# Left sums of a Strassen-type down-projection: on VectorE instead of accumulating transfers

## The chip, the cores and the metric

The kernel runs on one core of one Trainium2 chip. The metric is device microseconds of one execution, the median of three runs. One more execution was taken with the hardware profiler; its trace gives every row shown here.

## The reference, cut to what matters

One decoder block over 1024 tokens of width 1024 (`D_FF` is 2816), all in float32. The change lies in its last step, the down-projection of the gated MLP:

```python
h = rmsnorm(x, norm_ffn_g[l])
u = causal_dwconv(jnp.einsum("bsd,df->bsf", h, w_up[l]), conv_ffn_w[l])
gate_f, up_f = u[..., :D_FF], u[..., D_FF:]
x = x + jnp.einsum("bsf,fd->bsd", jax.nn.silu(gate_f) * up_f, w_down[l])
...
return rmsnorm(x, norm_final_g)
```

## The kernel before, in words

The kernel builds its instruction streams with a small list scheduler of its own: `Flow.run` holds threads, each of which yields the next instruction for one engine with a guessed duration and a rank; of the instructions that are ready when an engine comes free, the one of the lowest rank is emitted. What is emitted is then the fixed order of each engine's queue. Semaphores are set by the framework from that order, so an engine waits at an instruction until its inputs are there, and everything behind it in the same queue waits too.

`ffn_up` (up to line 1883) makes the 22 blocks of silu(gate) * up, each 128 features by 1024 tokens. ScalarE does the Silu (L1843), GpSimd multiplies by up (L1844), and SyncE stores the block in `act_dram` (L1846).

`ffn_down` multiplies those activations by `w_down`. It takes the 22 blocks in three groups of 6, 8 and 8. In a group the two operands are cut into 2 by 2 quarters, and the 8 quarter products are replaced by 7 products of sums of quarters (Strassen's method in Winograd's form). A quarter is 128 partitions by m feature blocks by 512, m being 3, 4 and 4 in the three groups, so it has 1536 or 2048 elements per partition.

- The left quarters come from the activations: A and B for the first 512 tokens, C and D for the last 512. The right quarters E, F, G, H come from `w_down`.
- The left sums are s1 (of C and D), s3 (of C and A), s2 (of A and s1) and s4 (of B and s2). The right sums are t1 to t4.
- The products are p1 = (A, E), p2 = (B, G), p6 = (s2, t2), p7 = (s3, t3), p5 = (s1, t1), p4 = (D, t4), p3 = (s4, H). TensorE does them in this order in every group (`order`, L1901). Before a product both factors are cut in two float32r parts (high and low): ScalarE copies the high part (L2031), VectorE subtracts it from the source for the low one (L2032), for two feature blocks at a time (1024 elements; 512 for the odd third block of the first group). The cut operands lie in `ht`, four places per side, that is two products' worth.
- A product is three matmuls (L374 to L376: low x high, high x high, high x low) per feature block and per 128 tokens: 36 matmuls in the first group and 48 in the others, 924 in all. The third of the three is the only one that reads the right factor's low part.
- The result of p1 is copied to the other four banks of PSUM before p2 adds to it (`seed`, L2080). Finished quarters are copied to the residual tiles x2 by ScalarE in the first group (L2091) or added to them by VectorE (L2096).

Right sums are made by VectorE (`rights`, L2004 and L2005). Left sums are made by transfers that add into their target, all from GpSimd's queue: `loaded` adds the second quarter to the one just loaded from DRAM (s1 and s3, L1979), and `lefts` adds s1 into the tile of A for s2, and s2 into the tile of B for s4 (L1988). Such a target can only be overwritten after its own cut. Loads of quarters go through SyncE's queue (L1971).

The block's own residual input is also added by accumulating transfers from GpSimd's queue: `residual` (L1945) has 16, of 256 KB each, one for each quarter of 128 tokens, and issues them while the first group runs. `finish` and `part` at the end of the kernel take the sum of squares, the final gain and the store.

Of the kernel before, what the change touches and what calls it, by code (L numbers as in the profile page):

```python
# [12 lines left out]
ALU = mybir.AluOpType  # L13
# [4 lines left out]
P = 128  # L18
# [4 lines left out]
H = 8  # L23
# [238 lines left out]
class Block:  # L262
# [1621 lines left out]
    def ffn_down(self, flow):  # L1884
# [13 lines left out]
        last = len(groups) - 1  # L1898
        x2, blocks, ops = [], {}, {}
        halves = [slice(0, 512), slice(512, 1024)]  # L1900
        order = ("p1", "p2", "p6", "p7", "p5", "p4", "p3")  # L1901
        base = dict(p1=0, p2=0, p6=4, p7=0, p5=4, p4=0, p3=4)
        target = dict(p2=(0, 0), p6=(4, 0), p7=(4, 1), p5=(4, 1), p4=(4, 0), p3=(0, 1))
        factors = dict(p1=("A", "E"), p2=("B", "G"), p6=("s2", "t2"), p7=("s3", "t3"), p5=("s1", "t1"), p4=("D", "t4"), p3=("s4", "H"))
# [32 lines left out]

        def residual():

            for p in ("p2", "p5", "p4", "p3"):  # L1940
                s0, half = target[p]
                for j in range(4):
                    yield On(("used", p, 0, j))
                    c = halves[half]
                    yield pool(1.0, lambda: gpsimd.dma_start(out=x2[s0 + j][:, c], in_=self.x2_dram[s0 + j][:, c], accum_op=ALU.add))  # L1945
                    flow.post(("x2", s0 + j, half), 4.0)
# [14 lines left out]

        def loads():
            for n, (_, _, m) in enumerate(groups):
                for name, (ready, src), more in (("A", left(n, 0, 0), None), ("E", right(n, 0, 0), None), ("B", left(n, 0, 1), None),
                                                 ("G", right(n, 1, 0), None), ("F", right(n, 0, 1), None), ("H", right(n, 1, 1), None),
                                                 ("s1", left(n, 1, 0), left(n, 1, 1)), ("s3", left(n, 1, 0), left(n, 0, 0)),
                                                 ("D", left(n, 1, 1), None)):
                    x = yield Get("blk")
                    t = self.m(f"blk{x}", P, m, 512)
                    yield On(*ready, *(more[0] if more else []))  # L1970
                    yield sp(0.75 * m, lambda: nc.sync.dma_start(out=t, in_=src))  # L1971
                    blocks[n, name] = x, t
                    flow.post(("load", n, name))
                    flow.fork(loaded(n, name, t, more), 0)

        def loaded(n, name, t, more):
# [3 lines left out]
                yield 4.0  # L1980
            flow.post(("block", n, name))

        def lefts(n):

            for to, x, y in (("s2", "A", "s1"), ("s4", "B", "s2")):
                yield On(("cut", n, x), ("block", n, y))
                o, src = blocks[n, x], blocks[n, y][1]
                yield pool(1.0, lambda: gpsimd.dma_start(out=o[1], in_=src, accum_op=ALU.add))  # L1988
                blocks[n, to] = o
                flow.post(("added", n, to))  # L1990
                yield 4.0
                flow.post(("block", n, to))

        def rights(n):
            m = groups[n][2]

            def op(to, o, x, y, fn):
                a, b = blocks[n, x][1], blocks[n, y][1]
                yield dve(512 * m, lambda: fn(o[1], a, b))
                blocks[n, to] = o  # L2000
                flow.post(("added", n, to))
                flow.post(("block", n, to))

            minus = lambda o, a, b: vector.tensor_tensor(out=o, in0=a, in1=b, op=ALU.subtract)  # L2004
            both = lambda o, a, b: vector.scalar_tensor_tensor(out=o, in0=a, scalar=-1.0, in1=b, op0=ALU.mult, op1=ALU.subtract)  # L2005
            yield On(("block", n, "F"), ("block", n, "H"))
            x = yield Get("blk")
            yield from op("t3", (x, self.m(f"blk{x}", P, m, 512)), "H", "F", minus)
            yield On(("block", n, "E"))
            yield from op("t1", blocks[n, "F"], "E", "F", minus)  # L2010
            yield On(("cut", n, "E"))
            yield from op("t2", blocks[n, "E"], "t1", "H", both)
            yield On(("cut", n, "G"), ("block", n, "G"))
            yield from op("t4", blocks[n, "G"], "t2", "G", both)


        later = dict(A="s2", B="s4", E="t2", G="t4")
# [1 line left out]

        def cuts(side):  # L2020
            for n, (_, _, m) in enumerate(groups):
                for p in order:
                    name = factors[p][side]
                    for k0 in range(0, m, 2):
                        x = yield Get(f"op{side}")
                        k = slice(k0, min(k0 + 2, m))
                        w = k.stop - k0
                        both = self.m(f"op{side}{x}", P, 2, 2, 512, dt=F32R)
                        yield On(("block", n, name))
                        src = blocks[n, name][1][:, k]  # L2030
                        yield act(w * 512, lambda: scalar.copy(out=both[:, 0, :w], in_=src))  # L2031
                        yield dve(w * 512, lambda: vector.tensor_tensor(out=both[:, 1, :w], in0=src, in1=f(both[:, 0, :w]), op=ALU.subtract))  # L2032
                        ops[n, p, k0, side] = x, both
                        flow.post(("op", n, p, k0, side))
# [15 lines left out]

        def products():
            for n, (_, _, m) in enumerate(groups):
                for p in order:
                    units = range(0, m, 2)
                    finest = n == last and p == "p3"
                    steps = [(k0, j) for j in range(4) for k0 in units] if finest else [(k0, j) for k0 in units for j in range(4)]
                    for k0, j in steps:
                        yield On(("op", n, p, k0, 0), ("op", n, p, k0, 1))
                        if k0 == 0:
                            yield On(bank_free(n, p, j))  # L2060
                        l, r = (ops[n, p, k0, side][1] for side in range(2))
                        ps = self.psum[:, base[p] + j, :]
                        w = min(2, m - k0)

                        def emit():
# [17 lines left out]
        def add(n, p, j):  # L2083

            s, half = target[p]
            s += j
            ps = self.psum[:, base[p] + j, :]
            if n == 0 and p in ("p2", "p6", "p7", "p3"):
                yield On("x2 places")
                o = x2[s][:, halves[half]]  # L2090
                yield act(540, lambda: scalar.activation(out=o, in_=ps, func=AF.Copy, scale=1.0 if s < 4 else -1.0))  # L2091
            else:
                if n:
                    yield On(("x2", s, half))
# [20 lines left out]

        def part(s, half, p, o, ss):
            ns = halves[half]
            yield On(("used", p, last, s % 4), "gain", *([("used", "p7", last, s % 4)] if s > 3 else []))
            flow.fork(squares(s, half, ss), 1)
            yield dve(560, lambda: vector.tensor_tensor(out=o[:, ns], in0=x2[s][:, ns], in1=self.gf[:, ns], op=ALU.mult))  # L2120
            yield On(("squares", s, half))
            flow.post(("part", s, half))
# [14 lines left out]

        def sides():
            for n in range(len(groups)):
                flow.fork(lefts(n), 1)  # L2140
                flow.fork(rights(n), 4 + n)
            yield 0.0

        def finishes():
            yield On(("used", "p7", last, 3))
            for s in (4, 5, 6, 7, 0, 1, 2, 3):
                flow.fork(finish(s), 2.5)

# [54 lines left out]
```

## Time and profile before

| what | value |
|---|---|
| median of three runs (2035.25 to 2039.29) | 2036.22 us |
| the profiled execution, as timed | 2038.57 us |
| its span from first to last instruction | 2036.8 us |
| TensorE busy, share of the span | 1982.9 us, 97% |
| VectorE busy | 1350.5 us, 66% |
| ScalarE busy | 906.2 us, 44% |
| GpSimd busy | 415.2 us, 20% |
| mean granted clock of TensorE | 0.988 of full speed |
| down-projection, first matmul to last | 1787.57 to 2029.35 us |
| software DMA queue (GpSimd's) | 22.81 MB, 5.1% of 16 engines |

Times in the trace are microseconds from the span's start. PE is TensorE, DVE VectorE, ACT ScalarE, POOL GpSimd, SP SyncE; a "q" behind an engine's name means its instruction queue. A tile is shown by the memory region that it lies in, not by its name in the program: of the left quarters of the first group A lies in `s5`, B in `s4`, C in `s3`, D in `w`; of the right ones E lies in `raw`, G in `s5`, F in `sb`, H in `s0`. A matmul's recorded duration includes its way through the array, so the next one starts before it ends; the step from start to start is what counts.

### The profile page before, as it was taken

Reading aid. Unit: us, or ns where it says so; the run is one execution under the profiler, and the core shown is the slowest. Engines: PE = TensorE matmul, PEld = TensorE weight load, DVE = VectorE, ACT = ScalarE, POOL = GpSimd, SP = SyncE. Lnnn points to the kernel's source line nnn. Section 1 sums busy time; section 2 is a strip of 40 time slices with the busy share of each in tenths; the row PEclk is TensorE's granted clock in tenths of the full one; section 3 lists DMA queues with packets and bytes.
Section 4 is the critical chain, followed back from the end, with each engine's and each line's share of the span. In section 5 each row is a group of like instructions: output and inputs, shape, how many; then the busy total and the mean of one; then the engine's idle time right before and its main releaser. Section 6 shows DMA issues by size and latency. Waiting matters only on the chain.

```text
span 2036.8 us, 27849 instructions
## 1 busy us (share of the span) xinstructions
PE 1982.9 (97%) x10645; PEld 1659.6 (81%) x10645; DVE 1350.5 (66%) x2488; ACT 906.2 (44%) x1936; POOL 415.2 (20%) x347
## 2 busy tenths in 40 slices
PE   9999999999999999999999999989999999968998
PEld 8987888888888888888888888867888888856787
DVE  7378678779778744666666332567777776756767
ACT  5265364464464334555454111344443443433435
POOL 3132021121120001010000022014445435322001
PEclk9999999999999999999999999999999999989999
DMA  6022311312312332101115543222322222299722
GB/s 213 33 75 50 90 43 47 86 40 49 85 40 50 104 116 72 36 26 37 56 47 180 163 135 106 91 73 73 109 72 88 89 73 91 76 278 247 212 58 83
DMA packets 204233, 187.99 MB, mean 92 GB/s; under 512 B 43418, under 2 KB 166020, under 8 KB 203588
## 3 DMA queue, kind: packets, MB, share of 16 engines
q1 hardware_dynamic: 189012, 150.75, 24.0%
q0 software_dynamic: 8032, 22.81, 5.1%
q10 hardware_dynamic: 7056, 12.65, 1.7%
q8 instruction: 84, 1.38, 0.3%
q14 instruction: 49, 0.40, 0.1%
HBM read 138.74 MB, written 41.68 MB: 89 GB/s over the span
## 4 chain that ended last, share of the span: by engine, by line
PE 90%; DMA 4%; DVE 3%; ACT 1%; issue 1%; POOL 0%; SPq 0%; POOLq 0%; ACTq 0%
PE psum L391 32%; PE psum L374 12%; PE psum L376 12%; PE psum L375 12%; PE psum L1394 5%; PE psum L489 3%; PE psum L1403 3%; DMA s<-s 2%; PE psum L1348 2%; PE psum L1568 1%; PE psum L1571 1%; PE psum L1570 1%; PE psum L679 1%; DMA s<-act_dram 1%; PE psum L871 1%; PE psum L905 1%
## 5 line engine op out<-in xcount | busy, mean ns | idle before, releaser
L391 PE MATMUL psum<-ht,w 128*128 128x512 f32 x2688 | 688.1, 400 | 0.1
L391 PEld LDWEIGHTS psum<-ht,w 128*128 128x128 f32 x2688 | 486.1, 189 | 89.8 <-DVE ht L1418 0.5
L374 PE MATMUL psum<-ht 128*128 128x512 f32 x308 | 122.2, 397 | 26.7 <-DVE ht L2032 15.0
L1860 DVE SCALAR_TENSOR_TENSOR s<-psum,cols,s 128x1023 f32<-128x1023 f32 (+1 forms) x88 | 106.8, 1275 | 54.7 <-ACT s L1857 54.7
L376 PE MATMUL psum<-ht 128*128 128x512 f32 x308 | 121.6, 395 | 0.3 <-DVE ht L2032 0.3
L375 PE MATMUL psum<-ht 128*128 128x512 f32 x308 | 121.6, 395 | 0.0
L636 DVE SCALAR_TENSOR_TENSOR s<-psum,cols,s 128x511 f32<-128x511 f32 (+1 forms) x144 | 105.3, 740 | 5.0 <-ACT s L631 4.8
L2032 DVE TENSOR_TENSOR ht<-s,ht 128x1024 fp32r<-128x1024 f32 (+1 forms) x60 | 66.7, 1139 | 51.0 <-ACT ht L2031 51.0
L2031 ACT CAST ht<-s 128x1024 fp32r<-128x1024 f32 (+1 forms) x60 | 57.0, 988 | 88.1 <-PE psum L376 53.6
L1844 POOL TENSOR_TENSOR s<-s 128x1024 f32<-128x1024 f32 x22 | 53.3, 2425 | 209.4 <-ACT s L1843 209.4
L374 PEld LDWEIGHTS psum<-ht 128*128 128x128 f32 x308 | 59.0, 192 | 39.8 <-DVE ht L2032 15.4
L766 DVE TENSOR_TENSOR s<-sc,s 64x240 f32<-64x240 f32 (+27 forms) x248 | 85.7, 346 | 5.6 <-DMA sc<-md_dram 1.1
L768 DVE TENSOR_TENSOR s<-s 64x240 f32<-64x240 f32 (+27 forms) x248 | 80.0, 323 | 5.9
L1857 ACT ACTIVATE s<-psum,cols 128x1024 f32<-128x1024 f32 x44 | 46.7, 1113 | 70.0 <-PE psum L376 70.0
L1328 DVE TENSOR_REDUCE nm<-psum 128x1 f32<-128x256 f32 (+5 forms) x64 | 48.3, 756 | 41.6 <-PE psum L1395 41.6
L374 PE MATMUL psum<-ht,w 128*128 128x512 f32 x168 | 66.4, 395 | 7.1 <-DVE w L1768 3.8
L623 DVE TENSOR_TENSOR w<-raw,w 128x512 fp32r<-128x512 f32 x96 | 65.4, 685 | 10.5 <-ACT w L621 10.4
L374 PE MATMUL psum<-ht,s 128*128 128x512 f32 x184 | 71.7, 390 | 0.4 <-DVE s L1768 0.4
L376 PE MATMUL psum<-ht,s 128*128 128x512 f32 x184 | 71.6, 389 | 0.0
L375 PE MATMUL psum<-ht,s 128*128 128x512 f32 x184 | 71.6, 389 | 0.0
L1483 POOL TENSOR_TENSOR s<-s 128x1024 f32<-128x1024 f32 x4 | 13.2, 3288 | 286.0 <-DMA rx<-in_w_o_mla_dram 260.6
L391 PE MATMUL psum<-s,w 128*128 128x512 f32 x288 | 69.9, 391 | 0.0
(456 smaller groups left out, 4742.4 us busy)
## 6 DMA issues: line engine op xcount, KB each, us to landing
raw<-in_w_in_dram SPq DMA_DIRECT2D x48, 512.0 KB, 4.2
raw<-in_w_up_dram SPq DMA_DIRECT2D x22, 512.0 KB, 3.7
act_dram<-s SPq DMA_DIRECT2D x22, 512.0 KB, 2.7
s<-in_x_dram SPq DMA_DIRECT2D x16, 512.0 KB, 3.6
sg_dram<-s ACTq DMA_DIRECT2D x16, 512.0 KB, 2.7
s<-sg_dram SPq DMA_DIRECT2D x16, 512.0 KB, 3.7
s<-act_dram SPq DMA_DIRECT2D x8, 1024.0 KB, 6.1
rx<-in_w_up_dram SPq DMA_DIRECT2D x11, 512.0 KB, 4.9
```

The source lines that it names most:

```text
L374: self.nc.tensor.matmul(ps, lhsT=ll, rhs=rh, start=first, stop=False, **kw)
L375: self.nc.tensor.matmul(ps, lhsT=lh, rhs=rh, start=False, stop=False, **kw)
L376: self.nc.tensor.matmul(ps, lhsT=lh, rhs=rl, start=False, stop=last, **kw)
L391: product = lambda o, l, r, **kw: pe(0.2155, lambda: self.nc.tensor.matmul(o, lhsT=l[:, k, :], rhs=r, **kw))
L489: yield pe(0.000417 * (b - a), lambda: tensor.matmul(ps[:, u, :b - a], lhsT=l[:, k, cs], rhs=w[:, k, a:b], start=n == 0, stop=n == 3 * KD ...
L623: yield dve(512, lambda: nc.vector.tensor_tensor(out=lo[:, c], in0=raw[:, c], in1=f(hi[:, c]), op=ALU.subtract))
L636: yield dve(570, lambda: nc.vector.scalar_tensor_tensor(out=o, in0=src[:, max(a - d, 0):b - d], scalar=self.cw[:, n, j:j + 1], in1=o, op0= ...
L766: yield dve(n * w, lambda: nc.vector.tensor_tensor(out=t, in0=mb[:, j, j + 1:].unsqueeze(2).to_broadcast(sh), in1=xb[:, j, :w].unsqueeze(1 ...
L768: yield dve(n * w, lambda: nc.vector.tensor_tensor(out=xb[:, j + 1:, :w], in0=xb[:, j + 1:, :w], in1=t, op=ALU.subtract))
L1394: nc.tensor.matmul(ps[:, n, :w], lhsT=l, rhs=r[:, n * w:(n + 1) * w], start=t == 0, stop=t == len(terms) - 1 and n != parts - 1)
L1860: yield dve(1160, lambda: vector.scalar_tensor_tensor(out=acc[:, d:], in0=src[:, :S - d], scalar=self.cf[:, n, j:j + 1], in1=acc[:, d:], o ...
L2032: yield dve(w * 512, lambda: vector.tensor_tensor(out=both[:, 1, :w], in0=src, in1=f(both[:, 0, :w]), op=ALU.subtract))
```

## The change

In the first group, C is loaded as it is, and VectorE makes all four left sums: s3 into a place of its own, s1 in place of C, s2 in place of A, s4 in place of B. In the other two groups s1 and s3 are still made by the accumulating transfers of `loaded`, and VectorE makes s2 and s4. The first group's product order becomes p1, p2, p7, p6, p5, p4, p3. The residual transfers start one group later: those of three quarters after the second group's last addition to that quarter, those of the fourth after p6 of the last group. Additions to x2 wait for them only in the last group, and `part` waits for them by name.

```diff
-        order = ("p1", "p2", "p6", "p7", "p5", "p4", "p3")
+        order = lambda n: ("p1", "p2", "p6", "p7", "p5", "p4", "p3") if n else ("p1", "p2", "p7", "p6", "p5", "p4", "p3")
...
-            for p in ("p2", "p5", "p4", "p3"):
-                s0, half = target[p]
+            for p, n, quarter in (("p2", last - 1, "p2"), ("p5", last - 1, "p5"), ("p3", last - 1, "p3"), ("p6", last, "p4")):
+                s0, half = target[quarter]
                 for j in range(4):
-                    yield On(("used", p, 0, j))
+                    yield On(("used", p, n, j))
...
+                sums = (("C", left(n, 1, 0), None),) if n == 0 else (("s1", left(n, 1, 0), left(n, 1, 1)), ("s3", left(n, 1, 0), left(n, 0, 0)))
...
+        def sum_steps(n, to, o, x, y, fn):
+            a, b = blocks[n, x][1], blocks[n, y][1]
+            yield dve(512 * groups[n][2], lambda: fn(o[1], a, b))
+            blocks[n, to] = o
+            flow.post(("added", n, to))
+            flow.post(("block", n, to))
...
         def lefts(n):
 
-            for to, x, y in (("s2", "A", "s1"), ("s4", "B", "s2")):
-                yield On(("cut", n, x), ("block", n, y))
-                o, src = blocks[n, x], blocks[n, y][1]
-                yield pool(1.0, lambda: gpsimd.dma_start(out=o[1], in_=src, accum_op=ALU.add))
...
+            if n == 0:
+                yield On(("block", n, "C"), ("block", n, "D"))
+                x = yield Get("blk")
+                yield from sum_steps(n, "s3", (x, self.m(f"blk{x}", P, groups[n][2], 512)), "C", "A", plus)
+                yield from sum_steps(n, "s1", blocks[n, "C"], "C", "D", plus)
+            yield On(("cut", n, "A"), ("block", n, "s1"), ("block", n, "s3"))
+            yield from sum_steps(n, "s2", blocks[n, "A"], "A", "s1", plus)
+            flow.fork(sum_after(n, "s4", "B", "s2", "B", plus), 7 + n)
...
-                if n:
+                if n == last and p != "p2" and not (p == "p6"):
                     yield On(("x2", s, half))
...
-            yield On(("used", p, last, s % 4), "gain", *([("used", "p7", last, s % 4)] if s > 3 else []))
+            yield On(("used", p, last, s % 4), ("x2", s, half), "gain", *([("used", "p7", last, s % 4)] if s > 3 else []))
...
-                flow.fork(lefts(n), 1)
+                flow.fork(lefts(n), 4 + n)
...
-            yield On(("used", "p7", last, 3))
+            yield On(("used", "p7", last, 3), ("used", "p6", last, 3))
```

VectorE's queue at the start of the first group, before. In the order of the rows: t3; the low part of G's first piece (`ht` from `s5`, 1024); t1; the low part of G's second piece (512); t2; t4; and the cuts of p6's factors, s2 (`s5`) and t2 (`raw`), which were reached by way of two transfers.

```order
L2004 TENSOR_TENSOR s2_13927<-s0_13911,sb_13896 128x1536
L2032 TENSOR_TENSOR ht_78<-s5_9852,ht_78 128x1024
L2004 TENSOR_TENSOR sb_13896<-raw_66,sb_13896 128x1536
L2032 TENSOR_TENSOR ht_78<-s5_9852,ht_78 128x512
L2005 SCALAR_TENSOR_TENSOR raw_66<-sb_13896,s0_13911 128x1536
L2005 SCALAR_TENSOR_TENSOR s5_9852<-raw_66,s5_9852 128x1536
L2032 TENSOR_TENSOR ht_78<-raw_66,ht_78 128x1024
L2032 TENSOR_TENSOR ht_78<-raw_66,ht_78 128x512
L2032 TENSOR_TENSOR ht_78<-s5_9852,ht_78 128x1024
```

The same place in the changed kernel, where sums are lines 1990 to 1992 and cuts line 2035:

```order
L1991 TENSOR_TENSOR s2_13927<-s0_13911,sb_13896 128x1536
L2035 TENSOR_TENSOR ht_78<-s5_9852,ht_78 128x1024
L1991 TENSOR_TENSOR sb_13896<-raw_66,sb_13896 128x1536
L1990 TENSOR_TENSOR w_13929<-s3_13928,s5_9852 128x1536
L1992 SCALAR_TENSOR_TENSOR raw_66<-sb_13896,s0_13911 128x1536
L1990 TENSOR_TENSOR s3_13928<-s3_13928,w_13929 128x1536
L2035 TENSOR_TENSOR ht_78<-s5_9852,ht_78 128x512
L1990 TENSOR_TENSOR s5_9852<-s5_9852,s3_13928 128x1536
L2035 TENSOR_TENSOR ht_78<-w_13929,ht_78 128x1024
L2035 TENSOR_TENSOR ht_78<-s2_13927,ht_78 128x1024
L1992 SCALAR_TENSOR_TENSOR s5_9852<-raw_66,s5_9852 128x1536
L2035 TENSOR_TENSOR ht_78<-w_13929,ht_78 128x512
```

Three sums (s3, t2, s1) now stand between t1 and the low part of G's second piece, which p2 needs, and a fourth (s2) stands between that and the first cuts of p7 (s3 in `w`, t3 in `s2`).

GpSimd's queue over the same time, before; L1979 and L1988 are the accumulating transfers of the left sums, L1945 those of the residual:

```order
L1979 DMA s3_13928<-act_dram_10711 128x3x512
L1844 TENSOR_TENSOR s4_9851<-s4_9851 128x1024
L1979 DMA w_13929<-act_dram_10711 128x3x512
L1988 DMA s5_9852<-s3_13928 128x1536
L1945 DMA s1_13930<-x2_dram_10710 128x512 x2
L1988 DMA s4_9851<-s5_9852 128x1536
L1945 DMA s1_13930<-x2_dram_10710 128x512 x2
L1979 DMA s3_13928<-act_dram_10711 128x4x512
L1945 DMA s1_13930<-x2_dram_10710 128x512 x2
L1945 DMA sc_13897<-x2_dram_10710 128x512
```

And in the changed kernel, from the last two products of `ffn_up` on:

```order
L1844 TENSOR_TENSOR s4_9851<-s4_9851 128x1024 x2
L1979 DMA sb_13896<-act_dram_10711 128x4x512
L1979 DMA w_13929<-act_dram_10711 128x4x512
L1945 DMA s1_13930<-x2_dram_10710 128x512 x4
L1979 DMA s5_9852<-act_dram_10711 128x4x512
L1945 DMA s1_13930<-x2_dram_10710 128x512
L1979 DMA s5_9852<-act_dram_10711 128x4x512
```

The two transfers of the second group's s1 and s3 stand directly behind the last product, with no residual transfer ahead of them.

## Rows read from the trace of the kernel before

**Rows 1.** Groups by line, 1786 to 2037 us: busy, mean ns, idle before, releasers

```profile
L374 PE MATMUL psum<-ht 128*128 128x512 f32 x308 | 122.2, 397 | 26.7 <-DVE ht L2032 15.0 <-ACT psum L2080 11.7
```

**Rows 2.** Timeline of TensorE: start, us, line, shape, [idle before <-releaser]

```profile
1787.57 0.39 PE L374 MATMUL psum<-ht 128*128 128x512 f32 x1
...
1796.63 0.50 PE L376 MATMUL psum<-ht 128*128 128x512 f32 x1 [0.28 <-DVE ht L2032]
...
1802.20 0.39 PE L376 MATMUL psum<-ht 128*128 128x512 f32 x1
...
1804.24 0.39 PE L376 MATMUL psum<-ht 128*128 128x512 f32 x1
...
2029.35 0.39 PE L376 MATMUL psum<-ht 128*128 128x512 f32 x1
```

**Rows 3.** Chain of work that ended last: start, us, what

```profile
1795.77 7.55 DMA s<-act_dram
...
1803.89 13.39 DMA s<-s
...
1859.97 23.39 DMA s<-s
```

**Rows 4.** Timeline of VectorE, first group, and one row of the second

```profile
1793.69 1.75 DVE L2004 TENSOR_TENSOR s<-s,sb 128x1536 f32<-128x1536 f32 x1
1795.36 1.22 DVE L2032 TENSOR_TENSOR ht<-s,ht 128x1024 fp32r<-128x1024 f32 x1
1796.49 4.67 DVE L2004 TENSOR_TENSOR sb<-raw,sb 128x1536 f32<-128x1536 f32 x1
1801.08 0.68 DVE L2032 TENSOR_TENSOR ht<-s,ht 128x512 fp32r<-128x512 f32 x1
1801.68 1.75 DVE L2005 SCALAR_TENSOR_TENSOR raw<-sb,s 128x1536 f32<-128x1536 f32 x1
1803.46 1.76 DVE L2005 SCALAR_TENSOR_TENSOR s<-raw,s 128x1536 f32<-128x1536 f32 x1
...
1855.94 4.62 DVE L2032 TENSOR_TENSOR ht<-s,ht 128x1024 fp32r<-128x1024 f32 x4
```

**Rows 5.** Timeline of GpSimd, two of the products of `ffn_up`

```profile
1775.80 2.41 POOL L1844 TENSOR_TENSOR s<-s 128x1024 f32<-128x1024 f32 x1 [10.18 <-ACT s L1843]
...
1796.65 2.89 POOL L1844 TENSOR_TENSOR s<-s 128x1024 f32<-128x1024 f32 x1
```

**Rows 6.** Timeline of ScalarE: the last Silu, and the cut behind the second wait

```profile
1794.42 1.06 ACT L1843 ACTIVATE s<-s 128x1024 f32<-128x1024 f32 x1
...
1883.46 1.99 ACT L2031 CAST ht<-s 128x1024 fp32r<-128x1024 f32 x2 [16.84 <-DMA s<-s]
```

**Rows 7.** Timeline of TensorE, two waits long before, at the start of `ffn_up`

```profile
1359.12 0.50 PE L374 MATMUL psum<-ht,w 128*128 128x512 f32 x1 [2.63 <-ACT psum L1796]
...
1367.04 0.47 PE L374 MATMUL psum<-ht,w 128*128 128x512 f32 x1 [3.77 <-DVE w L1768]
```

**Rows 8.** Busy by stretch: PE, PEld, DVE, ACT, POOL (x), granted clock, DMA share, GB/s

```profile
1364.00:1368.00 4.00, 0.96 (x4) 0.86 (x5) 3.96 (x4) 0.00 (x0) 2.27 (x2) 1.00 0.29 87
1368.10:1371.40 3.30, 3.30 (x9) 2.24 (x7) 2.58 (x6) 0.62 (x1) 0.00 (x0) 0.50 0.42 125
```

**Rows 9.** Line 2004 by shape: duration ns min/median/max, first and last start

```profile
L2004 DVE TENSOR_TENSOR sb<-w,s x1: 2292/2292/2292, 1838.6 to 1838.6; 128x2048 f32<-128x2048 f32 x1
```

**Rows 10.** Timeline of SyncE's queue: the load of the second group's C

```profile
1833.87 0.37 SPq L1971 DMA_DIRECT2D s<-act_dram  x1
```

**Rows 11.** Timeline of GpSimd: the transfer that adds D to it

```profile
1841.65 1.30 POOL L1979 DMA_DIRECT2D s<-act_dram  x1 [21.20 <-DMA s<-act_dram]
```

**Rows 12.** DMA issues, 1787 to 1900 us: KB each, median us from issue to landing

```profile
s<-x_dram POOLq DMA_DIRECT2D x12, 256.0 KB, 15.6
...
s<-act_dram POOLq DMA_DIRECT2D x1, 1024.0 KB, 9.1
```

**Rows 13.** VectorE busy in 20 us of the last group

```profile
1937.00:1957.00 20.00, 16.62 (x17) 1.00 0.37 73
```

More of the change, by code (lines that the diff above doesn't have):

```diff
@@ L1963, in loads @@
             for n, (_, _, m) in enumerate(groups):
+                sums = (("C", left(n, 1, 0), None),) if n == 0 else (("s1", left(n, 1, 0), left(n, 1, 1)), ("s3", left(n, 1, 0), left(n, 0, 0)))
                 for name, (ready, src), more in (("A", left(n, 0, 0), None), ("E", right(n, 0, 0), None), ("B", left(n, 0, 1), None),
-                                                 ("G", right(n, 1, 0), None), ("F", right(n, 0, 1), None), ("H", right(n, 1, 1), None),
-                                                 ("s1", left(n, 1, 0), left(n, 1, 1)), ("s3", left(n, 1, 0), left(n, 0, 0)),
+                                                 ("G", right(n, 1, 0), None), ("F", right(n, 0, 1), None), ("H", right(n, 1, 1), None), *sums,
                                                  ("D", left(n, 1, 1), None)):
@@ L1981, in loaded @@
             flow.post(("block", n, name))
-        def lefts(n):
-            for to, x, y in (("s2", "A", "s1"), ("s4", "B", "s2")):
-                yield On(("cut", n, x), ("block", n, y))
-                o, src = blocks[n, x], blocks[n, y][1]
-                yield pool(1.0, lambda: gpsimd.dma_start(out=o[1], in_=src, accum_op=ALU.add))
[L1989 to L1992, printed above, removed]
-        def rights(n):
[L1995 to L2005, printed above, removed]
+        def sum_steps(n, to, o, x, y, fn):
[4 more added lines that the diff above has]
+            flow.post(("block", n, to))
@@ new lines, in ffn_down @@
+        plus = lambda o, a, b: vector.tensor_tensor(out=o, in0=a, in1=b, op=ALU.add)
+        minus = lambda o, a, b: vector.tensor_tensor(out=o, in0=a, in1=b, op=ALU.subtract)
+        both = lambda o, a, b: vector.scalar_tensor_tensor(out=o, in0=a, scalar=-1.0, in1=b, op0=ALU.mult, op1=ALU.subtract)
+        def lefts(n):
+            if n == 0:
[6 more added lines that the diff above has]
+            flow.fork(sum_after(n, "s4", "B", "s2", "B", plus), 7 + n)
@@ L2006, in rights, with sum_after @@
+        def sum_after(n, to, x, y, waits, fn):
+            yield On(("cut", n, waits), ("block", n, x), ("block", n, y))
+            yield from sum_steps(n, to, blocks[n, waits], x, y, fn)
+        def rights(n):
             yield On(("block", n, "F"), ("block", n, "H"))
             x = yield Get("blk")
-            yield from op("t3", (x, self.m(f"blk{x}", P, m, 512)), "H", "F", minus)
+            yield from sum_steps(n, "t3", (x, self.m(f"blk{x}", P, groups[n][2], 512)), "H", "F", minus)
@@ L2009, in rights @@
             yield On(("block", n, "E"))
-            yield from op("t1", blocks[n, "F"], "E", "F", minus)
+            yield from sum_steps(n, "t1", blocks[n, "F"], "E", "F", minus)
             yield On(("cut", n, "E"))
-            yield from op("t2", blocks[n, "E"], "t1", "H", both)
-            yield On(("cut", n, "G"), ("block", n, "G"))
-            yield from op("t4", blocks[n, "G"], "t2", "G", both)
+            yield from sum_steps(n, "t2", blocks[n, "E"], "t1", "H", both)
+            flow.fork(sum_after(n, "t4", "t2", "G", "G", both), 7 + n)
@@ L2021, in cuts @@
             for n, (_, _, m) in enumerate(groups):
-                for p in order:
+                for p in order(n):
                     name = factors[p][side]
@@ L2052, in products @@
             for n, (_, _, m) in enumerate(groups):
-                for p in order:
+                for p in order(n):
                     units = range(0, m, 2)
```

## The prediction

> **What bounds the kernel now.** I read the groups by line first: the 308 matmuls of L374 that read `ht` from both sides, with as many of L375 and L376, are the 924 of the down-projection, and all that TensorE waited before them is 26.7 us, 15.0 for one cut of VectorE and 11.7 for one copy of ScalarE [rows 1]. Then the timeline of TensorE: between 1802.20 and 1804.24 lie 9 matmuls, so a step is 0.2267 us. The first down-projection matmul starts at 1787.57, the last at 2029.35 [rows 2], 241.8 us apart, while 923 steps take 209.2. So 32.5 us are lost in this stage: the 26.7, 0.3 at 1796.63, and about 5.5 of matmuls at the lower clock level after the two waits. What follows the last matmul is one tail of 7 us, which the change leaves alone.
>
> The chain of waits says where the two waits come from. For p6 of the first group, s1 is made by a transfer of 7.55 us and s2 by one of 13.39, one after the other [rows 3]; TensorE stands from 1804.47 to 1819.66. In the second group the transfer that makes s2 takes 23.39 us [rows 3], and ScalarE's cut of it [rows 6] stands in ScalarE's queue ahead of the four copies of p1 without which p2 can't start. TensorE bounds all the rest.
>
> **The change part by part.** Removed: all six transfers that make s2 and s4, the two that made s1 and s3 of the first group, and one load there (C, which was loaded twice). Both links of the first chain and the one of the second are among them. Added: eight sums on VectorE, four of 1536 and four of 2048 elements. A 1536 sum steps 1.67 us (1793.69 to 1795.36), its form with a scalar 1.78 and 1.68, a cut of 1024 elements 1.13, one of 512 0.60 [rows 4]; a 2048 sum takes 2.29 [rows 9]. I follow VectorE's new queue from 1793.69, before which nothing differs.
>
> t3 steps to 1795.36 and the low part of G's first piece to 1796.49, as now. t1 comes next. It now takes 4.67 us where its like takes 1.75, and it is the one sum that runs beside a GpSimd product [rows 4, 5]; it lost 2.9 us. That product still comes at this place, right behind the Silu that ends at 1795.48 [rows 6], and without the transfer that stands ahead of it now. Its 2.4 us [rows 5] are all that t1 can lose. From 1796.49 that gives 1796.49 + 2.4 + 1.7 = 1800.6 for t1's end. Then s3, t2 and s1 take 1.67 + 1.78 + 1.67 = 5.1, to 1805.7; C has landed by 1795.77 now, where the transfer that adds to it starts [rows 3], and D is loaded right behind it, so neither is late. Only then comes the low part of G's second piece, done at 1806.4. Now it starts at 1801.08 and is done at 1801.76 [rows 4], just ahead of the matmul at 1802.20 that reads it [rows 2], the third of p2's second piece. **So the change puts a new wait of 4.2 us into p2.** The ten matmuls left of p2 end at 1808.7. VectorE goes on with s2 (1.67, from 1806.3), the cut of s3 (done at 1809.2) and that of t3, done at 1810.3. p7's first matmul needs the one, its third the other, so the third starts at 1810.3.
>
> From there I find no further wait. p7 runs to 1818.0. Until then VectorE makes t4 (1.7), two cuts of 512 (1.2), s4 (1.7) and the cuts of s2 and t2 (2.3), to 1817.2; the second of these is needed 0.45 us after p6's start. This is the thinnest place. ScalarE empties p2's banks one by one as they end, before p7 comes to them, and p6's likewise before p5; I cost that at nothing, its queue being short here.
>
> In the second group s1 is still a transfer. C's load needs the place of t1, which is cut by 1823.4; load to issue of the transfer takes 7.8 us now [rows 10, 11] and the transfer 9.1 [rows 12], so s1 is there at 1840.3. VectorE comes to s2 at 1848 (p4's additions and the cuts of A and E stand ahead). s2 is ready at 1850.3, p6 starts at 1872.4; the wait for 23.39 is gone with its transfer. The third group has more time still. The residual moves behind p2, p5 and p3 of the second group and p6 of the last; its transfers took 15.6 us [rows 12], and p4's additions to the last quarter come 29 us after p6's. I cost it at nothing; that cover gone, each microsecond later delays the tail by one.
>
> **The sum.** p7's third matmul is number 75; 849 steps of 0.2267 follow it, 192.5 us. The last matmul starts at 1810.3 + 192.5 = 2002.8 against 2029.35: 26.6 us less. From it goes the lower clock. A wait of 3.77 us at 1367.04 [rows 7] was followed by 3.3 us at a granted 0.50, which began 1 us after TensorE had resumed [rows 8]; one of 2.63 [rows 7] had no such stretch behind it. Nine matmuls at half speed cost 1.8 us at most, and nothing while they wait for VectorE anyway, as p2's end does. I take 0.5, with bounds 0 and 1.8. That leaves 26.1 us. The profiled execution's 2038.57 becomes 2012.5; the median is 2.35 below it, so **2010 us**.
>
> Which of the two engines has the way to SBUF first is open. In the row, t1 started at 1796.49, 0.16 us before the product, and still lost 2.9 us [rows 4, 5]. By that, the product that starts at 1795.6 may also stop the cut that began at 1795.36; p2's third matmul would then wait 2.3 us longer, and the later wait shrinks to 1.9, because VectorE's total is the same. Two short waits, no lower clock: 2009.5. The Trainium skill ("SBUF — State Buffer", "SBUF: two separate sides") says that VectorE and GpSimd share a port pair as an exclusive lock, kept for the whole instruction by whichever starts first. By that rule the cut would end undisturbed, and there is one wait of 4.2 us: 2010. The row of t1 speaks against the second half of the rule.
>
> **The rivals.**
> First, VectorE's sums are all as slow as t1 was: s3, t2 and s1 each lose 2.9 us before G's second piece, 8.7 in all, and the clock costs its 1.8 in full: 2010 + 8.7 + 1.3 = 2020. It would take GpSimd work on SBUF between 1800 and 1806. For it: t1's row. Against it: GpSimd's new queue has nothing between the last product and the second group's transfers.
>
> Second, the wait moves into the second group: the transfer of s1 comes late, and VectorE stands at s2 with p2's cuts behind it. s2, t2 and two cuts take 2.3 + 2.3 + 2.3 us and p2 starts at 1861.5, so it decides from a landing at 1854.6, 23 us after its issue at 1831.2. For it: one transfer has taken 23.39 [rows 3]. Against it: that one stood behind residual transfers, this one behind none. Each microsecond beyond costs one; 5 would give 2015.
>
> Third, the other side: VectorE becomes the bound of the last two groups and the kernel is slower than before. In its densest stretch there VectorE is busy 16.62 of 20 us [rows 13]. A group is 7 products of 48 steps, 76.2 us, so 63.3 of work; with two more sums 67.9. Both groups together have 16.6 us to spare. To be slower than before it must grow by 16.6 + 26 = 43 us. That takes a loss like t1's 2.9 us at 15 of its instructions; the candidates are GpSimd's 20 transfers there, each if it blocked VectorE for 2.1 us while it is issued. Against it: four cuts took 4.62 us, 1.15 each and so undisturbed, while GpSimd issued a whole row of transfers at 1855.94 [rows 4]. Time if it all came: 2040.
>
> **How the numbers follow.** Forecast 0.85; first rival 0.06; second 0.04; third 0.03. The remaining 0.02 is for no difference: the gain found again as some wait that I don't see. About 0.2%, 4 us, is what a measurement of this kernel can tell from no change; the three runs lie 4 us apart. Faster by more than that: forecast and the first two rivals, 0.95; same 0.02; slower 0.03. The lower end: had t1 lost nothing, 2.4 us less, 2007.6; with the lowest run 1 us below the median, and 0.5 of clock given back, 2006. The upper end: full clock cost (1.3), p6's thin place missed by 2, highest run 3 above the median, 2016; and to take in most of the first rival, 2019.
>
> **What would show it.** Right: TensorE's two long waits gone, one of about 4 us for VectorE at 1802 to 1806 in p2, one of half a microsecond at p7; the last matmul about 26 us earlier; no L1988 transfers, s2 of the second group on VectorE before 1855. Wrong: a wait above 1 us for `ht` after p7 of the first group, a TensorE wait for ScalarE's copies (L2083), a sum other than t1 above 2.5 us, or a tail over 8 us.

## The result and the profile after

The changed kernel took 2013.18 us (median of four runs, 2011.96 to 2014.35), the kernel before 2037.76 beside it (2035.25 to 2040.40): a ratio of 0.9879, 95% interval 0.9862 to 0.9896. The profiled execution took 2012.15 us, its span is 2010.4.

The groups by line, the answer to [rows 1]: the 26.7 us of waiting before L374 are gone, and 4.0 stand before L376, all of it for cuts by VectorE (0.28 of it stood there before too [rows 2]).

```profile
L376 PE MATMUL psum<-ht 128*128 128x512 f32 x308 | 121.3, 394 | 4.0 <-DVE ht L2035 4.0
```

TensorE's timeline, the answer to [rows 2]:

```profile
1786.33 0.39 PE L374 MATMUL psum<-ht 128*128 128x512 f32 x1
...
1800.78 0.39 PE L375 MATMUL psum<-ht 128*128 128x512 f32 x1
1804.87 0.80 PE L376 MATMUL psum<-ht 128*128 128x512 f32 x1 [3.70 <-DVE ht L2035]
1805.46 0.63 PE L374 MATMUL psum<-ht 128*128 128x512 f32 x1
1805.89 0.63 PE L375 MATMUL psum<-ht 128*128 128x512 f32 x1
...
1810.15 0.62 PE L376 MATMUL psum<-ht 128*128 128x512 f32 x1
1810.58 0.43 PE L374 MATMUL psum<-ht 128*128 128x512 f32 x1
...
2002.87 0.39 PE L376 MATMUL psum<-ht 128*128 128x512 f32 x1
```

From the first down-projection matmul to the last are 216.54 us, 25.2 less than before. The stage also began 1.24 us earlier, which the change cannot touch (in e5, the same kernel again, it began at 1788.89). There is one new wait, in p2 (a step of 4.09 us), and twelve matmuls behind it step 0.43 us instead of 0.2267: the lower clock. The busy time by stretch (TensorE, its weight loads, VectorE, ScalarE, GpSimd, then the granted clock) shows it from 1803.8 on:

```profile
1786.30:1803.80 17.50, 14.58 (x63) 11.37 (x61) 16.12 (x10) 8.60 (x11) 3.27 (x1) 1.00 0.76 274
1803.80:1810.60 6.80, 5.73 (x14) 4.48 (x15) 6.62 (x6) 2.85 (x6) 0.00 (x0) 0.50 0.30 114
```

VectorE's timeline, the answer to [rows 4], holds the row of sums that makes TensorE wait, and s2 of the second group:

```profile
1794.12 1.22 DVE L2035 TENSOR_TENSOR ht<-s,ht 128x1024 fp32r<-128x1024 f32 x1
1795.26 3.95 DVE L1991 TENSOR_TENSOR sb<-raw,sb 128x1536 f32<-128x1536 f32 x1
1799.13 1.74 DVE L1990 TENSOR_TENSOR w<-s,s 128x1536 f32<-128x1536 f32 x1
1800.80 1.75 DVE L1992 SCALAR_TENSOR_TENSOR raw<-sb,s 128x1536 f32<-128x1536 f32 x1
1802.46 1.74 DVE L1990 TENSOR_TENSOR s<-s,w 128x1536 f32<-128x1536 f32 x1
1804.13 0.68 DVE L2035 TENSOR_TENSOR ht<-s,ht 128x512 fp32r<-128x512 f32 x1
...
1807.54 1.21 DVE L2035 TENSOR_TENSOR ht<-s,ht 128x1024 fp32r<-128x1024 f32 x1
1808.68 1.75 DVE L1992 SCALAR_TENSOR_TENSOR s<-raw,s 128x1536 f32<-128x1536 f32 x1
...
1847.97 2.28 DVE L1990 TENSOR_TENSOR s<-s,sb 128x2048 f32<-128x2048 f32 x1
```

Only t1 is long, and GpSimd's last product of `ffn_up` stands beside it (timeline of GpSimd, the answer to [rows 5]):

```profile
1794.32 3.27 POOL L1844 TENSOR_TENSOR s<-s 128x1024 f32<-128x1024 f32 x1 [17.35 <-ACT s L1843]
```

### The profile page after: what moved, and what is told of

Its sections match the earlier page's. It is cut to its first block, busy times and chain, and to the rows that moved or that the text cites. A ratio compares the mean times of both kernels' runs of the same rounds, so it can differ in the third digit from the quotient of the medians.

```text
span 2010.4 us, 27839 instructions
## 1 busy us (share of the span) xinstructions
PE 1978.5 (98%) x10645; PEld 1655.8 (82%) x10645; DVE 1363.8 (68%) x2496; ACT 907.3 (45%) x1936; POOL 409.1 (20%) x339
## 4 chain that ended last, share of the span: by engine, by line
PE 92%; DVE 4%; DMA 1%; ACT 1%; issue 1%; POOL 0%; SPq 0%; POOLq 0%; ACTq 0%; DVEq 0%
PE psum L391 32%; PE psum L374 12%; PE psum L376 12%; PE psum L375 12%; PE psum L1394 5%; PE psum L489 3%; PE psum L1403 3%; PE psum L1348 2%; PE psum L1568 1%; PE psum L1571 1%; PE psum L1570 1%; PE psum L679 1%; PE psum L871 1%; PE psum L905 1%; PE psum L915 1%; PE psum L873 1%
## 5 line engine op out<-in xcount | busy, mean ns | idle before, releaser
L376 PE MATMUL psum<-ht 128*128 128x512 f32 x308 | 121.3, 394 | 4.0 <-DVE ht L2035 4.0
L374 PE MATMUL psum<-ht 128*128 128x512 f32 x308 | 120.8, 392 | 0.0
L374 PE MATMUL psum<-ht,w 128*128 128x512 f32 x168 | 66.3, 395 | 7.1 <-DVE w L1768 3.8
L376 PEld LDWEIGHTS psum<-ht 128*128 128x128 f32 x308 | 58.5, 190 | 17.1 <-DVE ht L2035 4.8
L374 PE MATMUL psum<-ht,s 128*128 128x512 f32 x184 | 71.7, 390 | 0.4 <-DVE s L1768 0.4
L376 PE MATMUL psum<-ht,s 128*128 128x512 f32 x184 | 71.6, 389 | 0.0
```

What stands on the lines that cost most here:

```text
L374: self.nc.tensor.matmul(ps, lhsT=ll, rhs=rh, start=first, stop=False, **kw)
L376: self.nc.tensor.matmul(ps, lhsT=lh, rhs=rl, start=False, stop=last, **kw)
```

## The experiments

They ran on several chips, each beside the kernel before. "Stage" is the time from the first to the last matmul of the down-projection in the profiled execution: 241.78 us before, 216.54 after, so it leaves out what varies ahead of it. The kernel before has one profile, from one chip; so a stage's gain and the gain in time beside that run differ by up to 3.3 us (e2).

| run | us | ratio to before, 95% | stage, us |
|---|---|---|---|
| e1: only s2, s4 of groups 2 and 3 on VectorE | 2027.59 | 0.9931 (0.9917 to 0.9946) | 230.13 |
| e2: only the first group's part | 2043.81 | 1.0010 (1.0001 to 1.0020) | 247.11 |
| e3: only the residual later | 2027.06 | 0.9925 (0.9911 to 0.9940) | 229.07 |
| e4: the change, residual early | 2026.42 | 0.9925 (0.9910 to 0.9940) | 228.89 |
| e5: the change, again | 2014.23 | 0.9882 (0.9864 to 0.9901) | 216.43 |
| e6: the change, VectorE waits for the product | 2012.40 | 0.9868 (0.9854 to 0.9883) | 215.68 |
| e7: e4 with that wait | 2014.45 | 0.9876 (0.9862 to 0.9891) | 216.84 |
| e8: cuts first on VectorE | 2015.56 | 0.9882 (0.9868 to 0.9897) | 218.24 |
| e9: cuts first on VectorE and ScalarE | 2007.87 | 0.9846 (0.9833 to 0.9860) | 210.67 |
| e10: e2 with the wait of e6 | 2027.06 | 0.9941 (0.9928 to 0.9955) | 230.71 |
| e11: e4 again | 2013.13 | 0.9888 (0.9864 to 0.9912) | 216.39 |
| e12: e6 with p6 ahead of p7 | 2013.43 | 0.9868 (0.9852 to 0.9885) | 217.40 |

### Parts of the change alone: e1 to e4

e1, on the kernel before:

```diff
...
-                yield pool(1.0, lambda: gpsimd.dma_start(out=o[1], in_=src, accum_op=ALU.add))
+                if n == 0:
+                    yield pool(1.0, lambda: gpsimd.dma_start(out=o[1], in_=src, accum_op=ALU.add))
+                else:
+                    yield dve(512 * groups[n][2], lambda: plus(o[1], o[1], src))
...
-                flow.fork(lefts(n), 1)
+                flow.fork(lefts(n), 4 + n if n else 1)
```

> The kernel before, with only s2 and s4 of the second and third group made on VectorE; the first group keeps its two transfers, its order of products and its four sums by transfer, and the residual transfers stay where they were. Theory (the two gains are separate, each is its chain's): the second wait of 11.7 us, behind the transfer of 23.39, goes, and with it about 2 us of lower clock behind it; the wait of 15.0 us in the first group stays. So 13 to 14 us under the kernel before, about 2023, and the first group's waits unchanged within 0.5 us. Rival (the residual transfers are what is late): s1 of the second group, still a transfer behind residual transfers, now holds VectorE at s2, and a wait of more than 2 us stands at the second group's start: gain under 10 us.

e2 has all lines of the change's diff that concern `n == 0`, `loads`, `lefts` and the order, and none of those in `residual` and `add`; `lefts` of the later groups is as before.

> The kernel before, with only the first group's part of the change (C loaded as it is, four sums on VectorE, p7 ahead of p6); groups 2 and 3 make s2 and s4 by transfers, the residual transfers stay early. Theory: the first wait of 15.0 us and its lower clock of about 3 us go, and the changed kernel's own wait of 4.0 us in p2 and its lower clock of about 3 us come: 11 us under the kernel before, and the second wait stays at 8 to 14 us, because s2's transfer still stands behind twelve residual transfers. Rival: without the first wait everything ahead of the second group's s2 is earlier too, and the second wait shrinks below 5 us: 18 us or more under the kernel before.

e3 has only the lines of the diff in `residual`, `add`, `part` and `finishes`.

> The kernel before, with only the residual transfers moved one group later; all left sums are still transfers. Theory A (the 23.39 us of s2's transfer are mostly waiting behind residual transfers in the same queue): it takes about 9 us here, like the one of 1024 KB in the rows of before, and the second wait of 11.7 us goes: 11 to 14 us under the kernel before, as much as the VectorE sums of these two groups give. Theory B (the transfer from SBUF to SBUF is slow in itself): it takes over 18 us again and the wait stays above 6 us: under 6 us gained.

e4, on the changed kernel, takes those same lines of `residual` and `add` back.

> The changed kernel, with the residual transfers back where they were, one group earlier. Theory (the prediction's: VectorE's sums take the transfers out of the chain, the residual's place costs nothing either way): within 1.5 us of the changed kernel, 2013; s1 of the second group lands up to 1854, just in time. Rival: s1's transfer now stands behind the residual transfers and lands after 1855; VectorE waits at s2 with p2's cuts behind it, and TensorE waits 3 to 12 us at the second group: 2016 to 2025.

In e1 the second wait is gone and the time 14.2 us less, as expected; the first wait, which was to stay within 0.5 us, grew by 2.4. e3 did nearly as much, 14.7 us: the second group's s2 is still a transfer there, but with no residual transfer ahead of it in the queue it takes 10.6 us instead of 23.4 [rows 3], and the wait for it is gone (DMA issues of e3):

```profile
s<-s POOLq DMA_DIRECT2D x1, 1024.0 KB, 10.6
```

So the two parts are two cures for the same wait, and they do not add up. e2 and e4 went wrong: e2 gained nothing, e4 lost 12 us of stage against the change. Both show one thing that no theory of mine had, a GpSimd product of 21.91 us. In e4, GpSimd's timeline:

```profile
1796.90 21.91 POOL L1844 TENSOR_TENSOR s<-s 128x1024 f32<-128x1024 f32 x1 [17.34 <-ACT s L1843]
```

SyncE's queue, with the store of that product and the load that VectorE will wait for:

```profile
1818.84 0.33 SPq L1846 DMA_DIRECT2D act_dram<-s  x1
...
1831.60 2.49 SPq L1971 DMA_DIRECT2D raw<-in_w_down_dram  x1
```

VectorE's timeline, from the first cut of G to t3 of the second group:

```profile
1796.70 1.22 DVE L2035 TENSOR_TENSOR ht<-s,ht 128x1024 fp32r<-128x1024 f32 x1
1797.83 1.75 DVE L1991 TENSOR_TENSOR sb<-raw,sb 128x1536 f32<-128x1536 f32 x1
...
1815.86 0.69 DVE L2035 TENSOR_TENSOR ht<-s,ht 128x512 fp32r<-128x512 f32 x1
1817.01 2.35 DVE L2035 TENSOR_TENSOR ht<-raw,ht 128x512 fp32r<-128x512 f32 x1 [0.46 <-ACT ht L2034]
...
1845.85 2.29 DVE L1991 TENSOR_TENSOR s<-raw,s 128x2048 f32<-128x2048 f32 x1 [18.96 <-DMA raw<-in_w_down_dram]
```

And TensorE's timeline, in p4 of the first group:

```profile
1848.89 0.77 PE L374 MATMUL psum<-ht 128*128 128x512 f32 x1 [9.95 <-DVE ht L2035]
```

The product, which takes 2.41 us undisturbed [rows 5], takes 21.9. From the cut of G's first piece on VectorE runs sixteen instructions on SBUF without a gap, t1 at its undisturbed 1.75, and the product ends 2.3 us after VectorE's first pause begins, at 1816.55. Until then the block's store stands at the head of SyncE's queue with the next loads behind it. VectorE comes to the second group's t3, which needs one of them, and stands for 18.96 us; a cut for p4 stands behind t3, and TensorE waits 9.95 us.

In e3 the same product took 6.08 us, and it came in at a far smaller gap: VectorE's t2 ends at 1800.59, t4 starts at 1800.63, and t4 is the one that is long. (In e1 it was 5.9 us, in the same way. The wait at p6 of the first group, which both keep, is 2.4 and 2.5 us longer there than before. The transfer for s3 stands behind the product in GpSimd's queue and is issued at 1802.81 in e3, 1799.00 before; that this is the reason was not tested.) GpSimd's timeline in e3:

```profile
1796.78 6.08 POOL L1844 TENSOR_TENSOR s<-s 128x1024 f32<-128x1024 f32 x1
```

VectorE's timeline in e3:

```profile
1798.84 1.75 DVE L2005 SCALAR_TENSOR_TENSOR raw<-sb,s 128x1536 f32<-128x1536 f32 x1
1800.63 3.84 DVE L2005 SCALAR_TENSOR_TENSOR s<-raw,s 128x1536 f32<-128x1536 f32 x1
```

### Is the shut-out product the cause, and is it chance: e5 to e7, e10, e11

e5 and e11 are unaltered. e6, e7 and e10 have one more line ahead of t1 of the first group (and the scheduler's guess for the product shortened, so that all else keeps its order):

```diff
...
+            if n == 0:
+                yield On(("product", NF - 1))
+                yield dve(1, lambda: vector.tensor_copy(out=self.rowstat[:, 0, 0:1], in_=self.last_product[:, 0:1]))
             yield from sum_steps(n, "t1", blocks[n, "F"], "E", "F", minus)
```

> The changed kernel itself, unaltered, on another chip. Question: whether GpSimd's last product of the up stage (3.27 us beside VectorE in the first profile of this kernel, 21.9 us in the two runs whose VectorE had the same queue) is let in by chance. Theory A (which engine gets the port differs from chip to chip or from run to run): the product may take over 15 us here; then t1 takes 1.75, p2's wait is 1.9 instead of 4.1, SyncE's queue stands at the store of that product, the loads of the second group come 20 us later and TensorE waits about 10 us in p4 of the first group: 2020 to 2026. Theory B (the program alone decides): 3.27 us again, p2's wait 4.1, 2012 to 2015.

> The changed kernel with one instruction more: ahead of t1 VectorE copies one element per partition of the product, so it stands until GpSimd has finished. Theory (the loss is the product shut out by VectorE's unbroken row): the product starts as soon as the cut ahead of it ends and takes 3.3 us or less on any chip, the store leaves SyncE at about 1797.6, p2's wait is 4.1 to 4.4 us and there is no wait in p4: 2012 to 2016 whatever the changed kernel shows on the same chip. Rival (the wait is of no use, the product is slow for another reason): the product takes over 5 us, and VectorE waits for it: slower than the changed kernel by what it takes.

> The changed kernel with the residual transfers one group earlier and with the same wait of VectorE for the product. Theory A (in the run with early residual transfers, which gave 2026, the wait of 10 us in p4 came from the product of 21.9 us and the store behind it, the residual transfers are innocent): no wait in p4, 2012 to 2017. Theory B (the residual transfers in GpSimd's queue caused it): the wait of 10 us in p4 stays, or one of similar size at p1 or p2 of the second group, 2021 or more.

> The kernel with only the first group's part of the change, and with VectorE's wait for the last product of the up stage, so that this product can't be shut out. Theory (the gains of the first group and of the others are separate, and the missing gain of that part alone was the product of 21.9 us): the wait of 10 us in p4 goes; of the waits there stay 4.2 in p2 and one of 10 to 16 us at p2 of the second group, behind s2's transfer; 8 to 12 us under the kernel before. Rival (the first group's part gives nothing without the rest): within 4 us of the kernel before.

> The changed kernel with early residual transfers, without VectorE's wait, once more on another chip; its VectorE queue up to p7 of the first group is the changed kernel's own, instruction by instruction. Theory A (whether the product is shut out is fixed by the program, down to a few ns of its timing): 21.9 us again, 2024 to 2028. Theory B (it is the chip, or chance): 3.3 us and 2012 to 2016, like the changed kernel on two other chips.

With the wait the product takes 3.27 us in all three (and in e12, which has it too), and VectorE starts t1 on time behind it (VectorE in e6):

```profile
1800.15 0.15 DVE L2019 COPY rowstat<-s 128x1 f32<-128x1 f32 x1 [2.29 <-POOL s L1844]
1800.22 1.75 DVE L1994 TENSOR_TENSOR sb<-raw,sb 128x1536 f32<-128x1536 f32 x1
```

e7 settles the residual: early or late, with the product let in, 216.84 against e6's 215.68 and after's 216.54 of stage. e10 settles the first group: its part alone gives 11.1 us of stage (241.78 to 230.71) and 13.0 of time, and the second wait stays (TensorE in e10, groups by line):

```profile
L374 PE MATMUL psum<-ht 128*128 128x512 f32 x308 | 121.5, 394 | 12.8 <-ACT psum L2098 12.8
L376 PE MATMUL psum<-ht 128*128 128x512 f32 x308 | 121.3, 394 | 4.2 <-DVE ht L2050 4.2
```

e11 says that it is not the program alone: the kernel that gave 2025 to 2028 in all four runs of e4 gave 2012.98, 2012.98, 2013.28 and once 2024.59 on another chip, with 3.27 us for the product in its profile (GpSimd's timeline in e11):

```profile
1795.29 3.27 POOL L1844 TENSOR_TENSOR s<-s 128x1024 f32<-128x1024 f32 x1 [17.36 <-ACT s L1843]
```

e5 has 3.27 too, and one run of 2019.82 among three of 2012 to 2015. Those two high runs have no trace, so that the product was shut out in them is likely and not shown. What tips it stays open: in e4, e11 and after alike the product starts 0.20 us after the cut. The profiled executions speak for the chip: e1 to e4 ran on one, and the product was shut out in all four; on the others, without any added wait, it came in at once in after, e5 and e11, and in 2.89 us in the kernel before, whose VectorE queue is e3's over this stretch. The run of 2024.59, if it was shut out too, speaks for chance on one chip.

### A version that beats both: e8, e9, and the order alone: e12

e8 puts the remaining wait at its cause, the order of VectorE's queue. It also moves the last product from GpSimd to VectorE, where it takes 1.22 us, so that the collision goes with it; no run has the order without that. The condition lists for t1, t2 and s4 are lengthened in the same way as those shown:

```diff
+            if ft == NF - 1:
+                yield On(("op", 0, "p2", 0, 1))
+                yield dve(1024, lambda: vector.tensor_tensor(out=g, in0=g, in1=u, op=ALU.mult))
...
-                yield On(("block", n, "C"), ("block", n, "D"))
+                yield On(("block", n, "C"), ("block", n, "D"), ("cut", n, "G"))
...
+                yield On(("cut", n, "s3"),("cut", n, "t3"))
...
-            flow.fork(sum_after(n, "t4", "t2", "G", "G", both), 7 + n)
+            flow.fork(sum_after(n, "t4", "t2", "G", "G", both, [("cut", n, "t2"), ("cut", n, "s2")] if n == 0 else []), 7 + n)
```

> The changed kernel, with VectorE's queue of the first group in the order in which TensorE needs its results: the cuts of G's second piece and of p7's factors ahead of the sums t1, s1, t2, s2, t4 and s4 behind the cuts of p6's factors, and the last product of the up stage on VectorE behind the first cut of G instead of on GpSimd. Worked out with the trace's durations (1.13 for a cut of 1024 and for the product, 0.60 for a cut of 512, 1.67 a sum): G's second piece is cut at 1797.0 (needed 1801.1), p7's factors at 1801.5 (needed 1802.7), p6's at 1811.1 (needed 1810.8). So p2's wait of 4.1 us and the lower clock of 2.8 us behind it go, and about 0.3 us come at p6: 6 us under the changed kernel, 2007, and no product to be shut out. Rival (the four waits are only moved, because VectorE's total up to p6 is what bounds): a wait of 3 us or more at p7 or p6, and 2011 or more.

It missed: p2's wait went, and 1.9 us at p7 and 3.8 at p6 came. The reason is an engine I had left out, ScalarE. Its high part of s3 stood in the queue behind copies of p2's banks, which wait for TensorE (VectorE's timeline in e8):

```profile
1805.47 1.23 DVE L2040 TENSOR_TENSOR ht<-s,ht 128x1024 fp32r<-128x1024 f32 x1 [2.92 <-ACT ht L2039]
```

ScalarE's timeline in e8 over the same time, the copies first and then the high part:

```profile
1803.23 1.28 ACT L2099 ACTIVATE s<-psum 128x512 f32<-128x512 f32 x2 [3.68 <-PE psum L376]
1804.40 1.04 ACT L2039 CAST ht<-s 128x1024 fp32r<-128x1024 f32 x1
```

e9 is e8 with the copies held back:

```diff
-                yield On("x2 places")
+                first = {"p2": "p7", "p7": "p6"}.get(p)
+                yield On("x2 places", *[("op", n, first, k0, side) for k0 in (0, 2) for side in range(2) if first])
```

> The version with cuts first on VectorE, and now ScalarE's queue in the same order: the high parts of p7's factors stand ahead of the copies of p2's banks, those of p6's ahead of the copies of p7's. In the run before, VectorE waited 2.9 us for one such high part that stood behind two copies of p2's banks, which was the whole of the 1.9 us at p7, and 1.1 and 0.7 us for two more, part of the 3.8 us at p6. Theory (those two waits of TensorE come from ScalarE's order alone): at p7 0 to 0.4 us, at p6 0.4 to 1.2 us, no lower clock behind them; 5 to 6 us under the changed kernel, a ratio to the kernel before of 0.985 to 0.986. Rival (VectorE's total up to p6's cuts bounds): p6's wait stays at 2.5 us or more, a ratio of 0.987 or more.

All of it came: no wait at p7, one at p6 with a step of 0.94 us, and no matmul of the stage at the lower clock (TensorE in e9):

```profile
1813.05 0.39 PE L376 MATMUL psum<-ht 128*128 128x512 f32 x1
1813.99 0.50 PE L374 MATMUL psum<-ht 128*128 128x512 f32 x1 [0.55 <-DVE ht L2040]
```

2007.87 us is the fastest of all: of the 210.67 us of stage 209.2 are 923 steps at full clock. e9 against the changed kernel is a comparison through the kernel before: 0.9846 against 0.9879 and 0.9882, 0.9860 the upper end of the one and 0.9862 and 0.9864 the lower ends of the others. Against e6 (from 0.9854) the intervals overlap.

e12 changes the order of products in e6 back:

```diff
-        order = lambda n: ("p1", "p2", "p6", "p7", "p5", "p4", "p3") if n else ("p1", "p2", "p7", "p6", "p5", "p4", "p3")
+        order = lambda n: ("p1", "p2", "p6", "p7", "p5", "p4", "p3")
```

> The changed kernel with VectorE's wait for the last product, and with the old order of products in the first group, p6 ahead of p7. Theory (the order is worth what VectorE saves by not needing s2, t2 and their cuts right behind p2): the wait of 4.3 us in p2 stays, then s2's first cut comes 3 us after p2's end, because s2, t2's cut and t4 stand ahead of it, so a second wait of 2.5 to 3.5 us stands at p6's start; less what the lower clock no longer costs behind it, 1 to 3.5 us over the same kernel with the new order, a ratio to the kernel before of 0.988 to 0.989. Rival (the order is worth nothing, since VectorE is late for either): the same time, a ratio of 0.987 and no wait over 1 us at p6.

The wait at p6 is there, but its step is 1.61 us and not 3, since the lower clock already stretches the end of p2 to 1811.6. 217.40 us of stage against 215.68, and in the median no difference that can be measured (0.9868 both). In time the rival came, whose sign was a wait of at most 1 us at p6: the profile has 0.97 of idle time in that step. The new order is worth under 2 us here.

## Why the prediction was right, and what it missed

**The removed waits**: right. Both are gone; by the stages, e10 shows the first group's part to be worth 11 us and, against e6, the rest 15. The prediction counted the second wait once, and so it did not matter that the change removes it twice, by VectorE's sums (e1) and by the later residual (e3).

**The new wait in p2**: right. 4.2 us were forecast on top of the usual step; the step of 4.09 is 3.86 on top of it. t1 lost 2.2 of the 2.4 us; all other sums kept their 1.67.

**p7's wait and the lower clock**: the term for the clock was mis-sized. VectorE was ready for p7's third matmul 22.35 us after the stage's start (1808.68), forecast 22.7. TensorE issued it only at 1810.15, 23.82 us after the start, since p2's last and p7's first matmuls ran at half speed; with two slower steps behind it that makes 1.7 us, not 0.5 but near the upper bound of 1.8. The wait of half a microsecond at p7 is not to be seen, it lies under this. The step that failed is "nothing while they wait for VectorE anyway": the low clock reached past the point where VectorE was ready. The row that the term was taken from [rows 8] shows 3.3 us at the lower clock, after has 6.8. The length is not fixed by the wait: e6 has a step of 4.36 us in p2 and then 3.4 us at the lower clock with 7 slow steps, after 4.09 and 12 (busy time by stretch, e6):

```profile
1808.50:1811.90 3.40, 3.40 (x10) 2.62 (x9) 3.40 (x4) 1.80 (x4) 0.00 (x0) 0.51 0.03 10
```

**The sum**: stage 215.7 forecast, 216.54 measured, 0.4 less by VectorE and 1.2 more by the clock. The profiled execution took 2012.15, forecast 2012.5: the stage's 0.8 too many are hidden by its start, which came 1.24 us earlier, by no doing of the change. The median lies 3 us over the 2010 only because this profile lay 1 us below its median, and the one before 2.35 above.

**Second group and rivals**: right. The transfer of s1 took 11.1 us from its issue at 1829.51, landing at 1840.6, long before the second rival's 1854.6; VectorE came to s2 at 1847.97, forecast 1848. The first rival's slow sums did not come (1.74 and 1.75 us), and of the third's bound on VectorE there is no trace: TensorE waits nowhere behind p2 of the first group. The residual cost nothing (e7). The tail is 7.5 us, as before.

**Which engine has the port first**: the prediction weighed the rule of the Trainium skill ("SBUF — State Buffer", "SBUF: two separate sides"), an exclusive lock held for the whole instruction by whichever starts first, against the row of t1. In after the cut ended undisturbed at 1.22 us and the product took 0.86 more than its 2.41: the rule's case. The row of t1 before, which began 0.16 us ahead of the product and lost 2.9 us, was not followed up. Read by itself the rule would let no loser wait longer than one instruction of the other; the 21.9 us of e4 show that a row of instructions without a gap can hold it.

**What was not in it at all** is the other side of that collision. I asked what the product can cost t1, at most 2.4 us, and never what VectorE can cost the product. In e3, with the queue of before, VectorE's first gap, short as it is, comes behind four instructions, counted from the cut of G's first piece; the change makes it sixteen, and the product's store heads the queue of the loads. In e4 that cost 12 us of the change's 25: the second rival's kind of loss, by another way, not s1's transfer behind the residual but the loads behind one store. That the changed kernel came out at 2013 is luck in this respect: e4, whose VectorE queue is the same up to there, lay at 2025 to 2028 in four of four executions, above the range's 2019, and e5, the same kernel as after, has one execution at 2019.82. The row of t1 in the profile before was the sign that the two engines exclude each other, and I read it in one direction only.

## What to carry to other kernels

When a change fills an engine's last gaps, look for the instruction of the other engine that needed one, and for what stands in queues behind that; a cheap explicit wait (e6) makes such a stage independent of luck: in all four programs that had it the product took 3.27 us. When an engine becomes the late one, order its queue by when its reader needs each result, and then do the same on the engines that feed it: e8 without ScalarE gained nothing, e9 with it 6 us of stage (the product moved to VectorE included). And two cures of one wait are worth one of them: measure each part alone before crediting both.

## What was not expected of the hardware

A GpSimd product of 2.41 us on SBUF took 3.27, 6.08 or 21.91 us beside VectorE's instructions with two SBUF inputs: in the first it was let in behind the cut already running, in the others only at a gap of 0.04 us or of 0.46 us. Until then VectorE's instructions kept their usual length (1.75 us a sum), and the one that the product came in beside lost 1.7 us (the cut of 2.35 in e4) to 2.9 (t1 before). One program, e4 and e11, showed 21.91 on one chip and 3.27 on another. An accumulating transfer of 1 MB took 23.4 us behind residual transfers and 10.6 without them.
